# A small store of zeros to a scratch tensor, put on the DMA ring of the row stores

## Chip, cores, metric

One core of one Trainium2 chip. The metric is device time in microseconds (us), the median of several runs. All runs used here are of the fast state; repeats of one kernel mostly agree within 0.2%.

A ratio in this document is the mean time of one kernel's fast runs divided by the mean time of the other kernel's fast runs of the same rounds. It is therefore not quite the ratio of the medians that are quoted beside it. "Before" is run again in each set of rounds; its median was 165.10 to 165.27 us.

## The reference

Weights are adapted once (a low-rank update, then each column scaled to length `m`), and a large batch of rows is multiplied by them.

```python
batch, seq_len, in_dim, out_dim, rank = 16, 2048, 256, 256, 16
W_adapted = W + scale * (lora_A @ lora_B)
W_norm = np.sqrt(np.sum(W_adapted ** 2, axis=0, keepdims=True) + 1e-8)
W_final = W_adapted / W_norm * m
y = x.reshape(-1, in_dim) @ W_final          # 32768 x 256, float32
```

`x` and `y` are 33.6 MB each; the weights are small.

## The kernel before

Loads of W and x are issued by SyncE and go to one DMA ring (q1 in the profile). Loads of the small weights and all row stores are issued by ScalarE and go to another ring (q10). `x` comes in 8 blocks of 4 MB, 5 buffers deep; each partition's part of a block is one run of 32 KB.

```python
def load_x(b):                                    # SyncE's ring, q1
    t = xpool.tile([P, DJ, IN], FP32, name="x_sb", tag="x_sb")      # bufs=5
    nc.sync.dma_start(out=t, in_=x_flat[b * BLK : (b + 1) * BLK].rearrange("(p j) k -> p j k", p=P))
    return t

nc.scalar.dma_start(out=a_nat, in_=lora_A.rearrange("(c p) r -> p c r", p=P))   # ScalarE's ring, q10
nc.sync.dma_start(out=w_nat, in_=W.rearrange("(c p) o -> p c o", p=P))
nc.scalar.dma_start(out=b_nat, in_=lora_B)
nc.scalar.dma_start(out=m_row, in_=m[None, :])
# ... identity, ones, a warm-up of the square root table, then the weight chain:
nc.tensor.matmul(mb_ps, ones[0:1, :], m_row, start=True, stop=True)   # spreads m over the partitions
# ... lora_A @ lora_B, norm, w_final (bf16)

for b in range(NBLK):                             # 8 blocks
    x_sb = load_x(b)
    for c in range(DJ // J):                      # 8 chunks of a block
        # 8 transposes -> xt_ps; VectorE copies xt_ps to xt_sb (bf16); 8 matmuls -> y_ps
        nc.scalar.copy(out=x_sb[:, c * J : (c + 1) * J, :], in_=y_ps)      # result over the input
        if c + 1 in store_after[b]:               # after the block; thrice in the last one
            nc.scalar.dma_start(out=out_flat[...], in_=x_sb[:, j0:j_stored, :])   # q10 again
```

The sixth load of x needs the buffer of the first block, so it waits until the first row store has left. A row store goes out only when ScalarE has copied the block's last result.

## Time and profile before

| | before |
|---|---|
| time, median of 3 | 165.10 us |
| span of the profile | 163.3 us |
| bytes moved by DMA | 67.55 MB, 414 GB/s on average |
| busy share of TensorE, VectorE, ScalarE | 77%, 50%, 40% |
| last row store issued | 151.33 us |

The first view is the profile page of before: the mean busy share of the 16 DMA engines (tenths) and their rate in 40 slices of the span, and the DMA queues with packets, MB and their share of the time of 16 engines.

```profile
DMA  6999998999999899999999999999999999999992
GB/s 197 414 474 401 449 450 381 474 425 377 389 425 474 385 470 425 387 482 409 421 466 393 458 429 393 492 393 421 474 401 441 429 409 466 409 413 429 407 425 86
...
q1 hardware_dynamic: 1424, 33.82, 48.9%
q10 hardware_dynamic: 1746, 33.59, 48.0%
```

The engines of the DMA are at 9 (90% or more) almost from the start to the end, and two rings share them almost evenly. The table of windows says the same by stage (columns: window, length, busy time and count of each engine, TensorE clock, DMA share, GB/s):

```profile
17.00:151.00 134.00, 118.32 (x1012) 102.89 (x1010) 75.56 (x65) 63.83 (x64) 0.00 (x0) 1.00 1.00 427
151.00:163.00 12.00, 0.00 (x0) 0.00 (x0) 0.00 (x0) 0.30 (x1) 0.00 (x0) 0.65 0.74 313
```

Between 17 and 151 us the DMA share is 1.00, and TensorE is busy for 118 of 134 us. In the packet records of the trace one 32 KB packet takes 1.213 us at the median. Each engine has to move 64 of them in and the equivalent of 64 out: 128 x 1.213 = 155.3 us. That is an estimate of the floor of this kernel with these packets; the records of all its packets sum to 158.8 us per engine.

The chain of waits (shares of the span by engine, then by line) points elsewhere:

```profile
PE 57%; DVE 26%; DMA 4%; issue 2%; ACT 1%; DVEq 1%; ACTq 1%
```

It follows compute back from ScalarE's last copy. How far that is from the end of the kernel is shown by two fences: the timeline (start, length, engine, line, operation), then the table of DMA issues (count, KB each, us from issue to landing):

```profile
150.28 1.01 ACT L165 COPY x_sb<-y_ps 128x1024 f32<-128x1024 f32 x1
151.33 0.34 ACTq L170 DMA_DIRECT2D out_dram<-x_sb  x1
```

```profile
out_dram<-x_sb ACTq DMA_DIRECT2D x2, 1024.0 KB, 11.0
```

Compute ends at 151.3 us. The last two row stores, 1 MB each, take 11.0 us at the median to land, because other stores are still in the rings ahead of them: by the packet records 3.8 MB are moved after 151.33 us. Compute is ahead of the end of the stores by about 11 us, here called the backlog.

The start, from the timeline of before:

```profile
1.22 3.29 SPq L52 DMA_DIRECT2D x_sb<-in_x_dram  x5
1.78 0.53 ACTq L66 DMA_DIRECT2D m_row<-in_m_dram  x1
2.34 1.28 ACT L76 ACT_TABLE_LOAD   x1 [2.34 <-issue]
8.96 1.19 PE L91 MATMUL mb_ps<-m_row,ones 1*128 1x256 f32 x2 [4.58 <-DMA m_row<-in_m_dram]
14.03 3.67 PE L147 MATMUL xt_ps<-identity,x_sb 128*128 128x128 f32 x16
```

The bias row `m_row` is issued at 1.78 us and its matmul can begin only at 8.96 us: its packets take turns with 32 KB packets of x on the same engine.

### The profile page before, as it was taken

To read this page: it belongs to the slowest core of one execution; us is meant where nothing else is said; L and a number is where in the kernel's file an instruction comes from. 1 tells how busy PE (TensorE), PEld (TensorE's weight loads), DVE (VectorE), ACT (ScalarE), POOL (GpSimd) and SP (SyncE) were. 2 spreads that over 40 slices of the span, in tenths; PEclk is the share of its full clock that TensorE was granted. 3 is DMA by queue.
4 is the path that set the end of the run, shared out by engine and by line. 5 is a ranking of instruction groups with operands and counts; after the bars stand their busy time and mean duration, and the time that the engine had idled before them with its cause. 6 is when DMAs were issued, how large, how long until landed. Compare 5 with 4: busy or idle time off the path is not lost.

```text
span 163.3 us, 2370 instructions
## 1 busy us (share of the span) xinstructions
PE 125.4 (77%) x1034; PEld 107.9 (66%) x1034; DVE 81.1 (50%) x76; ACT 66.1 (40%) x67; POOL 0.7 (0%) x6
## 2 busy tenths in 40 slices
PE   0049888888888888888888888898889888886000
PEld 0028677777777777777778777777887777774000
DVE  0145755555555555554555455545554555455000
ACT  3001244443544444444444364427441844085000
POOL 1000000000000000000000000000000000000000
PEclk9999999999999999999999999999999999999955
DMA  6999998999999899999999999999999999999992
GB/s 197 414 474 401 449 450 381 474 425 377 389 425 474 385 470 425 387 482 409 421 466 393 458 429 393 492 393 421 474 401 441 429 409 466 409 413 429 407 425 86
DMA packets 3180, 67.55 MB, mean 414 GB/s; under 512 B 593, under 2 KB 866, under 8 KB 866
## 3 DMA queue, kind: packets, MB, share of 16 engines
q1 hardware_dynamic: 1424, 33.82, 48.9%
q10 hardware_dynamic: 1746, 33.59, 48.0%
q8 instruction: 8, 0.13, 0.3%
q14 instruction: 2, 0.02, 0.0%
HBM read 33.85 MB, written 33.55 MB: 413 GB/s over the span
## 4 chain that ended last, share of the span: by engine, by line
PE 57%; DVE 26%; DMA 4%; issue 2%; ACT 1%; DVEq 1%; ACTq 1%
PE y_ps L158 33%; DVE xt_sb L153 23%; PE xt_ps L147 22%; DMA m_row<-in_m_dram 4%; PE n_ps L115 1%; DVE rnorm L124 1%; DVEq L206 1%; PE mb_ps L91 1%; ACT x_sb L165 1%; DVE w_final L126 0%; DVE sq L110 0%; DVE wa L106 0%; ACTq L60 0%; ACTq L64 0%; ACT norm L119 0%
## 5 line engine op out<-in xcount | busy, mean ns | idle before, releaser
L153 DVE CAST xt_sb<-xt_ps 128x1024 bf16<-128x1024 f32 x64 | 75.4, 1220 | 56.6 <-PE xt_ps L147 42.2
L165 ACT COPY x_sb<-y_ps 128x1024 f32<-128x1024 f32 x64 | 64.1, 1013 | 72.5 <-PE y_ps L158 72.4
L158 PE MATMUL y_ps<-w_final,xt_sb 128*128 128x256 bf16 x512 | 65.5, 273 | 11.5 <-DVE xt_sb L153 11.5
L147 PE MATMUL xt_ps<-identity,x_sb 128*128 128x128 f32 x512 | 68.7, 279 | 3.4 <-DVE xt_sb L153 3.1
L147 PEld LDWEIGHTS xt_ps<-identity,x_sb 128*128 128x128 f32 x512 | 58.7, 144 | 7.8 <-DVE xt_sb L153 6.7
L158 PEld LDWEIGHTS <-xt_sb 128*128 128x128 bf16 x512 | 47.8, 98 | 22.8 <-DVE xt_sb L153 18.2
L91 PE MATMUL mb_ps<-m_row,ones 1*128 1x256 f32 x2 | 1.2, 694 | 4.6 <-DMA m_row<-in_m_dram 4.6
L119 ACT ACTIVATE norm<-n_ps,eps_col 128x256 f32<-128x256 f32 x1 | 0.5, 473 | 10.4 <-PE n_ps L115 10.4
L91 PEld LDWEIGHTS mb_ps<-m_row,ones 1*128 1x128 f32 x2 | 0.5, 304 | 5.0 <-DVE aT L88 5.0
L82 DVE CAST b_bf<-b_nat 16x256 bf16<-16x256 f32 x1 | 0.3, 280 | 6.5 <-DMA b_nat<-in_lora_B_dram 6.5
L86 PE MATMUL aT_ps<-identity,a_nat 128*16 128x128 f32 x2 | 0.6, 394 | 3.8 <-DMA a_nat<-in_lora_A_dram 3.8
L115 PE MATMUL n_ps<-sq,ones 128*128 128x256 f32 x4 | 2.1, 674 | 1.5 <-DVE sq L110 1.5
L124 DVE RECIPROCAL rnorm<-norm 128x256 f32<-128x256 f32 x1 | 1.8, 1753 | 2.0 <-ACT norm L119 2.0
L86 PEld LDWEIGHTS aT_ps<-identity,a_nat 128*16 128x16 f32 x2 | 0.1, 88 | 3.8 <-issue 3.8
L115 PEld LDWEIGHTS n_ps<-sq,ones 128*128 128x128 f32 x4 | 1.2, 323 | 2.2 <-DVE sq L110 2.0
L76 ACT ACT_TABLE_LOAD x1 | 1.3, 1283 | 2.3 <-issue 2.3
L93 DVE COPY m_all<-mb_ps 128x256 f32<-128x256 f32 x1 | 0.4, 424 | 2.1 <-PE mb_ps L91 2.1
L126 DVE TENSOR_TENSOR w_final<-wam,rnorm 128x256 bf16<-128x256 f32 x2 | 0.8, 424 | 0.0
L122 DVE TENSOR_TENSOR wam<-wa,m_all 128x256 f32<-128x256 f32 x2 | 0.8, 418 | 0.0
L110 DVE TENSOR_TENSOR sq<-wa 128x512 f32<-128x512 f32 x1 | 0.7, 693 | 0.0
L106 DVE SCALAR_TENSOR_TENSOR wa<-ab_ps,w_nat 128x512 f32<-128x512 f32 x1 | 0.7, 692 | 0.0
L97 PE MATMUL ab_ps<-b_bf,aT 16*128 16x256 bf16 x2 | 0.6, 416 | 0.0
(11 smaller groups left out, 2.0 us busy)
## 6 DMA issues: line engine op xcount, KB each, us to landing
x_sb<-in_x_dram SPq DMA_DIRECT2D x8, 4096.0 KB, 31.2
out_dram<-x_sb ACTq DMA_DIRECT2D x7, 4096.0 KB, 27.9
out_dram<-x_sb ACTq DMA_DIRECT2D x1, 2048.0 KB, 12.4
out_dram<-x_sb ACTq DMA_DIRECT2D x2, 1024.0 KB, 11.0
w_nat<-in_W_dram SPq DMA_DIRECT2D x1, 256.0 KB, 2.8
a_nat<-in_lora_A_dram ACTq DMA_DIRECT2D x1, 16.0 KB, 2.9
b_nat<-in_lora_B_dram ACTq DMA_DIRECT2D x1, 16.0 KB, 6.2
m_row<-in_m_dram ACTq DMA_DIRECT2D x1, 1.0 KB
```

The lines of the kernel that those rows point to most:

```text
L76: nc.scalar.activation(out=warm, in_=eps_col, func=AF.Sqrt)
L86: nc.tensor.transpose(aT_ps[:, c * P : (c + 1) * P], a_nat[:, c, :], identity)
L91: nc.tensor.matmul(mb_ps, ones[0:1, :], m_row, start=True, stop=True)
L115: nc.tensor.matmul(n2_ps, ones, sq[:, c, :], start=(c == 0), stop=(c == KC - 1))
L122: nc.vector.tensor_mul(out=wam[:, c], in0=wa[:, c], in1=m_all)
L124: nc.vector.reciprocal(out=rnorm, in_=norm)
L126: nc.vector.tensor_mul(out=w_final[:, c], in0=wam[:, c], in1=rnorm)
L147: nc.tensor.transpose(xt_ps[:, kc, j * P : (j + 1) * P], x_sb[:, c * J + j, kc * P : (kc + 1) * P], identity,)
L153: nc.vector.tensor_copy(out=xt_sb, in_=xt_ps)
L158: nc.tensor.matmul(y_ps[:, j, :], xt_sb[:, kc, j * P : (j + 1) * P], w_final[:, kc, :], start=(kc == 0 and (j % (J // 2)) == 0), stop=(kc ...
L165: nc.scalar.copy(out=x_sb[:, c * J : (c + 1) * J, :], in_=y_ps)
L206: with _tile.TileContext(nc) as tc:
```

## The change

An internal scratch tensor gets 128 rows of 64 B of zeros, stored by ScalarE just behind the load of `m_row`. Nothing reads it. The question is what a small extra DMA costs when it is put on a ring that later carries the row stores.

```diff
     nc.scalar.dma_start(out=b_nat, in_=lora_B)
     m_row = startup.tile([1, OUT], FP32)
     nc.scalar.dma_start(out=m_row, in_=m[None, :])
+
+    scratch = nc.dram_tensor("scratch", (P, 16), FP32, kind="Internal").ap()
+    mark = startup.tile([P, 16], FP32)
+    nc.vector.memset(mark, 0.0)
+    nc.scalar.dma_start(out=scratch, in_=mark)
```

## The prediction

> **What bounds the kernel now.** The DMA engines, not the compute. A table of windows gives a DMA share of 1.00 in every window from 17 to 151 us. The queue table splits it: 48.9% for the ring of the loads (q1), 48.0% for the ring of the row stores (q10). In the packet records a 32 KB packet takes 1.213 us at the median; each of 16 engines moves 64 of them for the loads and the equivalent of 64 for the stores: 128 x 1.213 = 155.3 us of a span of 163.3. The chain of waits names TensorE and VectorE instead, because it follows compute back from the last copy; but that copy ends at 151.3 us and 12 us follow in which only stores drain (last store issued at 151.33, landing 11.0 us later). So compute ends with a DMA backlog of 11 us: a few us of delay in compute are hidden.
>
> **What the change adds.** One VectorE memset of 128x16 (the 128x1 one took 0.06 us), one ScalarE DMA issue (0.49 to 0.53 us for its neighbours), and a store of 128 rows of 64 B: 8 small packets and a semaphore packet per engine. It removes nothing.
>
> 1. The ScalarE table load, at 2.34 us, moves by about 0.5 us. ScalarE's next need is at 14.19 us: free.
> 2. The store stands behind the bias-row load m_row; that still lands at about 8.8 us.
> 3. DMA time: 64 B reads of lora_A took 0.011 us each, semaphore packets 0.009: together 0.1 us of each engine. Writes may cost more: the Trainium skill (DMA: Bandwidth & Descriptors, Specifications) says that under 512 B the engine does read-modify-write; no run shows a small write yet. At 0.05 us each (what a 1 KB packet took) it would be 0.45 us, an estimate. As DMA is the limit, this counts in full.
> 4. The store takes turns with x packets (same page, Queues, rings and completion order: engines switch rings at packet boundaries). b_nat's data ran at about 4.5 us, its semaphore packets one x packet later. If each small packet takes a turn of 1.2 us, the store lands near 18 us; if all 8 go together, near 10. No one waits for it.
> 5. The rotation of DMA semaphores shifts by one. The fifth load of x would wait for lora_B (landed by 7.5 us) instead of W. Over 12 MB of loads are queued before it: free. Later reuse falls on transfers long landed.
>
> The row stores begin at 34.1 us, long after. What is left is the order of turns: one engine's last semaphore packet comes 1.16 us behind the next; another phase could move that end by some tenths of a us either way.
>
> **Predicted:** 165.3 us, 8 times in 10 between 164.7 and 166.1. Chances: faster by over 2% 0.01, within 2% 0.97, slower by over 2% 0.02.
>
> **Right, if** DMA share is still 1.00 between 17 and 151 us, 32 KB packets still take 1.213 us, m_row lands within 0.3 us of 8.8, the first x chunk starts at 14.0, compute ends at about 151.3, and the store's packets add under 0.5 us per engine. **Wrong, if** m_row or the first x load lands over 1 us later, a load of x is held up by the scratch store, or engines idle anew.
>
> **What would make it wrong.** The scratch tensor moving the outputs in memory so that packets take another time; 64 B writes that hold an engine for a microsecond each (+9 us); a semaphore shift that makes a load wait for a store in flight; or a phase shift worth more than 1.2 us.

## The result

| | before | after |
|---|---|---|
| median | 165.13 us (4 runs) | 165.17 us (4 runs) |
| ratio, 95% interval | | 1.000, 0.9983 to 1.0017 |
| span of the profile | 163.3 us | 163.4 us |
| `m_row` matmul starts | 8.96 us | 9.92 us |
| last row store issued | 151.33 us | 152.25 us |

The profile page of after, the same lines as of before:

```profile
DMA  6999999999999999899999999999999999999992
GB/s 197 430 474 386 465 433 393 477 409 377 393 397 489 393 457 437 385 483 409 413 465 393 473 421 393 481 411 413 465 401 449 437 401 465 417 413 417 421 413 88
...
q1 hardware_dynamic: 1424, 33.82, 48.9%
q10 hardware_dynamic: 1890, 33.60, 48.1%
```

q10 has 144 packets more: 128 rows and 16 semaphore packets. The windows:

```profile
17.00:151.00 134.00, 118.51 (x1016) 103.40 (x1014) 76.46 (x67) 63.00 (x63) 0.00 (x0) 1.00 1.00 427
151.00:163.00 12.00, 0.17 (x2) 0.00 (x0) 0.00 (x0) 1.11 (x2) 0.00 (x0) 0.62 0.75 320
```

The DMA share is 1.00 again and the rate 427 GB/s again. The packet records give 1.213 us as the median of a 32 KB packet, as before, and 0.011 us for each row of the scratch store, 0.09 us in all per engine.

The chain of waits of after is that of before but for 5% instead of 4% of DMA, the late `m_row`:

```profile
PE 57%; DVE 26%; DMA 5%; issue 2%; ACT 1%; DVEq 1%; ACTq 1%
```

The start, the last copy, the last row store and the landing of the scratch store (timeline, then table of DMA issues):

```profile
1.22 6.77 SPq L52 DMA_DIRECT2D x_sb<-in_x_dram  x5
2.35 0.36 ACTq L73 DMA_DIRECT2D scratch<-mark  x1
2.74 1.28 ACT L83 ACT_TABLE_LOAD   x1 [2.74 <-issue]
9.92 1.19 PE L98 MATMUL mb_ps<-m_row,ones 1*128 1x256 f32 x2 [5.54 <-DMA m_row<-in_m_dram]
14.91 3.15 PE L154 MATMUL xt_ps<-identity,x_sb 128*128 128x128 f32 x16
...
151.21 1.01 ACT L172 COPY x_sb<-y_ps 128x1024 f32<-128x1024 f32 x1
152.25 0.34 ACTq L177 DMA_DIRECT2D out_dram<-x_sb  x1
```

```profile
scratch<-mark ACTq DMA_DIRECT2D x1, 8.0 KB, 17.1
out_dram<-x_sb ACTq DMA_DIRECT2D x2, 1024.0 KB, 10.1
```

Three things are to be seen. The scratch store took 17.1 us to land. The five loads of x take until 7.99 us to issue instead of 4.51 (start plus length of the merged line), as the fifth waits for `lora_B`. And all of compute came 0.9 to 1.0 us later than before, from the matmul of `m_row` to the last row store, yet the kernel ended at the same time: the backlog at the end took it up.

The late `m_row` was not predicted. It had to be tested whether the store causes it.

### The profile page after: what moved, and what is told of

The parts are those of the page before. It is cut to its first block, busy times and chain, and to the rows that moved or that the text cites. A ratio compares the mean times of both kernels' runs of the same rounds, so it can differ in the third digit from the quotient of the medians.

```text
span 163.4 us, 2373 instructions
## 1 busy us (share of the span) xinstructions
PE 124.8 (76%) x1034; PEld 107.8 (66%) x1034; DVE 81.1 (50%) x77; ACT 66.1 (40%) x67; POOL 0.7 (0%) x6
## 4 chain that ended last, share of the span: by engine, by line
PE 57%; DVE 26%; DMA 5%; issue 2%; ACT 1%; DVEq 1%; ACTq 1%
PE y_ps L165 33%; DVE xt_sb L160 23%; PE xt_ps L154 22%; DMA m_row<-in_m_dram 5%; PE n_ps L122 1%; DVE rnorm L131 1%; DVEq L213 1%; PE mb_ps L98 1%; ACT x_sb L172 1%; DVE w_final L133 0%; DVE sq L117 0%; DVE wa L113 0%; ACTq L60 0%; ACTq L64 0%; ACT norm L126 0%
```

## The experiments

Theory D: the DMA engines are the limit, so added DMA time counts in full, and delays of compute count only beyond the backlog, which was taken to be some 11 us (too much, as will be seen). Rival C: the chain of waits is right, compute is the limit, and every microsecond of a late weight chain counts. Beside these, theories L and S on the late `m_row`, and theories on what small packets do to the ring.

### The two kernels again

The kernel before and the change, unedited, each against before.

> The change itself again, unedited, for its noise and for one question: in the first profile of the change the bias row m_row landed 0.97 us later than before (start of its matmul 9.92 us instead of 8.96). Theory L (lottery): the engine that carries m_row was one of the few whose lora_B packet came one x packet late, which is decided before the scratch store is on the ring, so in a repeat the matmul can start near 8.9 or near 9.9. Theory S (store): the scratch store makes it late, so it starts at 9.7 to 10.1 again. Both: ratio 0.998 to 1.003, 165.1 us, since the delay is absorbed by the DMA backlog at the end.

> The kernel before, unedited, against itself, with a second profile: how far the start of m_row's matmul moves without any scratch store (8.96 us in the first profile). Theory L: it can be anywhere from 8.9 to 10 us. Theory S: 8.8 to 9.1 us. Time ratio 0.998 to 1.002.

Measured: the change again 165.22 us (ratio 0.9998, 0.9985 to 1.0011), before again 165.27 us (0.9999, 0.9985 to 1.0013). The timeline of the change again:

```profile
8.89 1.19 PE L98 MATMUL mb_ps<-m_row,ones 1*128 1x256 f32 x2 [4.18 <-DMA m_row<-in_m_dram]
...
151.22 0.34 ACTq L177 DMA_DIRECT2D out_dram<-x_sb  x1
```

With the same code the matmul started at 8.89 us, and the last row store was issued at 151.22 us instead of 152.25. Before again had its matmul at 9.19 us. In the six other profiles with a scratch store behind `m_row` on that ring, described below, it started at 8.78, 9.11, 8.91, 8.91, 8.71 and 8.83 us. Only one of eight such profiles is near 9.9, so theory S falls: the store does not delay `m_row` by 1 us. In the packet records of the first profile of the change, `m_row`'s own packet ran at 8.09 us instead of 6.9 to 7.2 us as in the other seven and in the first profile of before, one turn with an x packet later. That fits theory L: the packet follows by 1.22 us a semaphore packet of `lora_B` at 6.87 us, one of three late ones of 16, and such late packets occur without the store too (three in the first profile of before, none in the second). What decides which engine is late was not tested, nor whether the store makes a late one more frequent.

The two profiles of the change are also a test of theory D by accident: compute ended 1.03 us apart, and the profiled executions took 165.18 and 165.14 us.

### The store ahead of the bias row

```diff
     nc.scalar.dma_start(out=b_nat, in_=lora_B)
+    scratch = nc.dram_tensor("scratch", (64, 16), FP32, kind="Internal").ap()   # (128, 16) in ahead_full
+    mark = startup.tile([64, 16], FP32)                                         # [128, 16] in ahead_full
+    nc.vector.memset(mark, 0.0)
+    nc.scalar.dma_start(out=scratch, in_=mark)
     m_row = startup.tile([1, OUT], FP32)
     nc.scalar.dma_start(out=m_row, in_=m[None, :])
```

> The store, cut to 64 rows of 64 B, is issued ahead of m_row instead of behind it, so that m_row waits on the ring for 4 small packets and a semaphore packet, 5 turns of 1.22 us = 6.1 us. Both theories: m_row's matmul starts at about 15 us instead of 8.96, and the last row store is issued at about 157.4 us instead of 151.3. Theory D (the DMA engines are the limit, 11 us of backlog at the end of compute): the time stays within 0.5% of before, 164.9 to 165.9 us, and the tail after the last copy shrinks from 12 to about 6 us. Theory C (the chain of waits is right, compute is the limit): +6 us, about 171 us.

> The full 8 KB store ahead of m_row: 9 turns, about 11 us. m_row's matmul starts at about 20 us, the last row store is issued at about 162.3 us. Theory D: the backlog of about 11 us is used up; the last 1 MB store needs some 2.4 us of transfer plus about 2 us of issue and landing, so the time is about 168 to 170 us (+2 to +3%). Theory C: +11 us, about 176 us. If small packets took no turns, m_row would not move at all and the time would be 165.1 us.

| | `m_row` matmul starts | last row store issued | median | ratio, 95% interval |
|---|---|---|---|---|
| before (first profile) | 8.96 us | 151.33 us | 165.23 us | |
| half, 4 rows per engine | 13.93 us | 157.85 us | 166.13 us | 1.0050, 1.0023 to 1.0077 |
| full, 8 rows per engine | 18.71 us | 161.04 us | 169.84 us | 1.0302, 1.0268 to 1.0335 |

Of the half version, its matmul of `m_row`, its last row store and the landing of the last two row stores (timeline, then DMA issues):

```profile
13.93 1.19 PE L96 MATMUL mb_ps<-m_row,ones 1*128 1x256 f32 x2 [9.46 <-DMA m_row<-in_m_dram]
...
157.85 0.34 ACTq L175 DMA_DIRECT2D out_dram<-x_sb  x1
```

```profile
out_dram<-x_sb ACTq DMA_DIRECT2D x2, 1024.0 KB, 6.1
```

The windows of the full version, then its matmul of `m_row`, its last row store and the landings in the same way:

```profile
17.00:151.00 134.00, 116.12 (x966) 101.10 (x967) 75.52 (x68) 58.62 (x59) 0.00 (x0) 1.00 0.97 412
151.00:163.00 12.00, 7.99 (x69) 6.44 (x67) 4.71 (x4) 5.98 (x6) 0.00 (x0) 0.98 0.93 392
```

```profile
18.71 1.19 PE L96 MATMUL mb_ps<-m_row,ones 1*128 1x256 f32 x2 [14.24 <-DMA m_row<-in_m_dram]
...
161.04 0.34 ACTq L175 DMA_DIRECT2D out_dram<-x_sb  x1
```

```profile
out_dram<-x_sb ACTq DMA_DIRECT2D x2, 1024.0 KB, 6.2
```

What stands behind small packets on a ring waits for them, by turns: 9 turns (8 rows and a semaphore packet) cost `m_row` 9.8 us, 5 turns cost 5.0 us, so 1.0 to 1.1 us for a turn on average. In the packet records a turn with an x packet is 1.22 us; one turn, at about 13.0 us, falls to the short semaphore packet of the first load of x instead, so both delays are about 1 us less than expected. The order of the change (behind `m_row`) is what made it free. Of 6.5 us by which the end of compute moved in the half version, 0.9 us reached the time; of 9.7 us in the full version, 4.6 us did. Rival C asked for all of it, so C falls, and a backlog is shown. But it hid only 5.6 and 5.1 us, not 11. The fences say why: with compute late, the last two row stores still took 6.1 and 6.2 us at the median to land, so some 5 of the 11.0 us were usable (11.0 - 6.1 = 4.9, an estimate from these landings). In the full version the DMA share in the window from 17 to 151 us falls to 0.97: the engines now wait for compute at times.

The half version missed the expected range by 0.2 us, and its runs spread from 165.33 to 166.91 us. Counting in the packet records how many of the 16 engines are busy, the engines idle 0.55 us on average from 133 to 143 us, where before they idle not at all. So some of the backlog is needed earlier than at the very end. That spread from run to run is open.

### The same store on the other ring, and as one packet

`sp_ring` issues the store from SyncE, ahead of the first load of x. `one_packet` keeps it on ScalarE's ring but shapes the same 8 KB as 16 rows of 512 B, one packet per engine.

```diff
-    nc.scalar.dma_start(out=scratch, in_=mark)
+    nc.sync.dma_start(out=scratch, in_=mark)                 # sp_ring
```

```diff
-    scratch = nc.dram_tensor("scratch", (P, 16), FP32, kind="Internal").ap()
-    mark = startup.tile([P, 16], FP32)
+    scratch = nc.dram_tensor("scratch", (16, 128), FP32, kind="Internal").ap()   # one_packet
+    mark = startup.tile([16, 128], FP32)
```

> The same 8 KB store on the other ring, that of the loads, between W and the first load of x. There are no x packets ahead of it with which to take turns. If turns made it land 17.1 us after issue, it lands here within 5 us of issue; if small writes to memory are slow in themselves, it lands late here too. The first load of x may move by some tenths of a us. Time 164.8 to 165.6 us, same.

> The same 8 KB laid out as 16 rows of 512 B: one packet and one semaphore packet per engine, 2 turns instead of 9. Landing about 8.5 us earlier than in the change: some 8 us after issue instead of 17.1. Time the same, 164.8 to 165.5 us, as nobody waits for it.

The landings, first of sp_ring, then of one_packet (tables of DMA issues):

```profile
scratch<-mark SPq DMA_DIRECT2D x1, 8.0 KB, 2.9
```

```profile
scratch<-mark ACTq DMA_DIRECT2D x1, 8.0 KB, 8.7
```

The landing is 2.9 us where no x packet is in the way, 8.7 us with 2 turns, 17.1 us with 9 turns (16.1 us in the change again, where `m_row` was not late). A small write to memory is not slow by itself here; the turns make it late. The Trainium skill (DMA: Bandwidth & Descriptors, Queues, rings and completion order) says that an engine changes between rings at packet boundaries. This agrees, and it shows that each 64 B row was a packet of its own: in the records of the change, successive rows on one engine start about 1.22 us apart.

The time of one_packet was 165.03 us (ratio 0.9987, 0.9974 to 1.0001), the same. The time of sp_ring was 166.56 us (ratio 1.0065, 1.0037 to 1.0093), outside its expected range, although the weights now came early. Its timeline:

```profile
1.72 3.47 SPq L52 DMA_DIRECT2D x_sb<-in_x_dram  x5
4.54 1.22 PE L98 MATMUL mb_ps<-m_row,ones 1*128 1x256 f32 x2
15.46 3.67 PE L154 MATMUL xt_ps<-identity,x_sb 128*128 128x128 f32 x16 [5.70 <-DMA x_sb<-in_x_dram]
```

The matmul of `m_row` starts 4.4 us earlier than before and gains nothing, as theory D says. But the first load of x is issued 0.5 us later (1.72 instead of 1.22 us), and the first chunk of x starts 1.4 us later (15.46 instead of 14.03). By the packet records the engines idled 0.55 us on average in the 10 us after the first x packet, where before they did not idle, and the 32 KB packets took 0.5 us more per engine in all. So the likely cause is a late start of the DMA, which a backlog of stores at the end cannot cover; that this makes the whole rise was not shown. Why the runs spread from 165.33 to 166.85 us is open.

### The dose by bytes

```diff
-    scratch = nc.dram_tensor("scratch", (P, 16), FP32, kind="Internal").ap()
-    mark = startup.tile([P, 16], FP32)
+    scratch = nc.dram_tensor("scratch", (P, 1024), FP32, kind="Internal").ap()   # wide_4k: 512 KB
+    mark = startup.tile([P, 1024], FP32)
```

> The dose by bytes: 512 KB again, but as 128 rows of 4 KB: 8 packets per engine of about 0.155 us (half of the 0.309 us of an 8 KB packet) in place of 8 of 0.011. Theory D: +1.2 us minus what was there, 166.1 to 166.6 us, 0.6 to 0.9% slower. If there is slack on the DMA engines: no change, 165.1 us.

Measured: 166.38 us against 165.25 (ratio 1.0067, 1.0054 to 1.0081). The DMA queues of its page:

```profile
q1 hardware_dynamic: 1424, 33.82, 48.6%
q10 hardware_dynamic: 1890, 34.11, 48.5%
```

The 8 packets of each engine took 0.159 us each at the median, 1.27 us in all by the records; the medians differ by 1.13 us. Here the added DMA time counts in full within the noise, as theory D says, and there is no slack on the DMA engines. Compute also ended 0.9 us later than before (last row store issued at 152.19 us), but in the first profile of the change the same delay cost nothing.

### The dose by packets

The 64 B of zeros per partition are stored k times, to a scratch tensor k times as large: 8k small packets per engine. The first of these runs was `many_64`.

```diff
-    scratch = nc.dram_tensor("scratch", (P, 16), FP32, kind="Internal").ap()
+    scratch = nc.dram_tensor("scratch", (P, 64, 16), FP32, kind="Internal").ap()     # k = 64; also 16, 8, 3
-    nc.scalar.dma_start(out=scratch, in_=mark)
+    nc.scalar.dma_start(out=scratch, in_=mark[:, None, :].to_broadcast([P, 64, 16]))
```

> The dose by packets: the scratch tensor is 128 x 64 rows of 64 B (512 KB), the same 64 B of zeros per partition stored 64 times, so 512 small packets per engine instead of 8. Theory D with the cost seen (11 ns a packet, 13 ns pitch where two ran back to back): +6.7 us, about 171 to 173 us. If a 64 B write holds an engine for 0.05 us (read-modify-write felt by the engine): +25 us. The packets take turns with x packets until the first five loads are done at about 48 us, so the first row store, in order behind them on the ring, moves little before about 50 us instead of starting at 34.

> The dose by packets again, a quarter of it: 16 rows of 64 B per partition, 128 small packets per engine. With 64 rows the time rose by 14.3 us, twice the 6.7 us expected, and ScalarE's issue of the first row store took 24.0 us instead of 0.37. Theory B (blocked issue): the packets cost about 13 ns each, and the rest came from ScalarE standing still in that issue, so that compute ended 19 us late. Then 128 packets cost 1.6 us (166.6 to 167.2 us) as long as the issue of the first row store stays under 1 us; if that issue takes many us too, the time goes up by more. Theory P (packets cost more than they show, about 28 ns each): +3.5 us, about 168.7 us, with the last row store issued at about 151 us.

> 8 rows of 64 B per partition: 64 small packets per engine. At 34.1 us some 42 of them are left, and they take turns with x packets until the loads end at about 51 us. Either way the first row store cannot move before that. Theory Q (waiting in the ring costs little, only a held ScalarE costs): if the issue of the first row store is not held (0.4 us), compute ends at about 151 us and the time is 165.5 to 167 us; if it is held until about 51 us as with 16 and 64 rows, compute ends at about 163 us and the time is 171 to 173 us. Theory W (the wait of the row store behind small packets is itself the cost): 171 to 173 us also where the issue is not held.

> 3 rows of 64 B per partition: 24 small packets and a semaphore packet per engine, 25 turns of 1.22 us from about 7 us, so the last one runs at about 38 us, just past 34.1 us, where ScalarE issues the first row store. That store then waits a few us on the ring behind the small packets. Expected: the time stays within 0.5% of before, 165.0 to 166.0 us, because the loads of x fill the engines meanwhile. If the issue itself is held, ScalarE stands still for up to 4 us and compute ends up to 4 us later, which the backlog of 11 us still covers.

| k | small packets per engine | issue of the first row store takes | last row store issued | median | ratio, 95% interval |
|---|---|---|---|---|---|
| 1 (the change) | 8 | 0.37 us | 152.25 us | 165.17 us | 1.0000, 0.9983 to 1.0017 |
| 3 | 24 | 0.38 us | 151.06 us | 165.30 us | 1.0008, 0.9996 to 1.0020 |
| 8 | 64 | 0.39 us | 151.20 us | 165.32 us | 1.0012, 0.9999 to 1.0025 |
| 16 | 128 | 17.26 us | 163.63 us | 172.73 us | 1.0453, 1.0429 to 1.0477 |
| 64 | 512 | 24.02 us | 170.82 us | 179.54 us | 1.0860, 1.0836 to 1.0883 |

ScalarE's timeline around its first row store, first with k = 8, then with k = 16:

```profile
33.98 0.39 ACTq L177 DMA_DIRECT2D out_dram<-x_sb  x1
35.85 1.01 ACT L172 COPY x_sb<-y_ps 128x1024 f32<-128x1024 f32 x1 [1.90 <-PE y_ps L165]
```

```profile
34.06 17.26 ACTq L177 DMA_DIRECT2D out_dram<-x_sb  x1
51.42 1.93 ACT L172 COPY x_sb<-y_ps 128x1024 f32<-128x1024 f32 x2 [17.39 <-issue]
```

The issue of the scratch store itself, with k = 16, then with k = 64:

```profile
2.34 0.59 ACTq L73 DMA_DIRECT2D scratch<-mark  x1
```

```profile
2.35 0.58 ACTq L73 DMA_DIRECT2D scratch<-mark  x1
```

With k = 8 the row store is issued in 0.39 us and ScalarE goes on copying. The store itself moves its first packet only at 52.5 us, by the packet records, where before that was at 37.7 us, because it stands behind small packets that take turns with x. This wait of 15 us costs nearly nothing (+0.1%): the loads of x fill the engines meanwhile. With k = 16 the issue instruction lasts 17.26 us, to 51.32 us. By then nearly all packets of the first five loads of x had started; 87 of 128 small packets per engine were still left, and most of them went at once from 52 to 53 us. With k = 64 the issue ended only at 58.08 us, when the small packets were down to 5 of 512. ScalarE copies nothing in that time, compute ends 12.3 us later than before (163.63 against 151.33), and the backlog is spent. So a wait in the ring is free here and a held ScalarE is not. Theory B (blocked issue) and theory Q say the same. Theory P (28 ns for each packet) and theory W (the ring wait is the cost) fall: k = 8 shows both 64 packets and the ring wait for 0.1%. In its records the small packets take 0.7 us per engine; less than that reached the time (0.07 us, at most 0.4 by the interval), and part of it ran at once with other packets of the same engine. The run with k = 3 does not test the wait: its small packets were done at 34.1 us, not at about 38 as expected.

The Trainium skill (Perfetto Trace Analysis, DMA Instruction — HWDGE) says that the instruction lasts until all of its descriptors have been generated, and that there is a buffer for them which can fill. A full buffer could explain a held issue, but this agrees only in part. By that account the scratch store itself, with its many rows, should be the long instruction; yet its issue took 0.58 us with k = 8 and k = 64 and 0.59 us with k = 16, and the hold fell on the next DMA that ScalarE issued. When that was issued, at about 34 us, 39 small packets per engine were left with k = 8 (not held), 103 with k = 16 and 487 with k = 64 (held). If the number left is what counts, the limit lies between 39 and 103. The ends of the two held issues (87 left, 5 left) don't fit one count, and what exactly is full stays open.

The sum for k = 16, per engine and from the packet records, against before: small packets 1.4 us, idle 4.9 us more, 32 KB packets 1.4 us more; 7.7 us together, for a rise of 7.5 us from the first x packet to the last packet (some packets of one engine run at once, so such sums come out a little high). For k = 64 the expectation of 6.7 us had left out the held issue, and the measured rise was 14.3 us: by the records small packets 8.9 us (a mean of 17 ns, a median of 11), of which some 3.7 us at once with other packets of the same engine, idle 7.9 us more, 32 KB packets 1.4 us more. Why the 32 KB packets took longer is open. The backlog hid about 5 us here too: compute ended 12.3 and 19.5 us later, the time rose by 7.5 and 14.3 us.

### The many packets from GpSimd

```diff
-    nc.scalar.dma_start(out=scratch, in_=mark[:, None, :].to_broadcast([P, 64, 16]))
+    nc.gpsimd.dma_start(out=scratch, in_=mark[:, None, :].to_broadcast([P, 64, 16]))   # many_64_pool
```

> The store of 512 small packets per engine issued from GpSimd, on neither of the two rings, so that no row store stands behind it and ScalarE cannot be held by it. Theory B: ScalarE's issue of the first row store stays near 0.37 us at about 34 us, compute ends at about 151 us, and the time rises by the packets alone, by 5.6 to 6.7 us if they are as small as on the ScalarE ring (171 to 172 us), or less if this path joins them. Theory P: again about +14 us.

Measured: 167.68 us against 165.19 (ratio 1.0147, 1.0128 to 1.0166). ScalarE's issue took 0.38 us again, and the last row store was issued at 153.46 us instead of 170.82. That is theory B's part that a store on a third ring cannot hold ScalarE. The price of 512 small packets could not be read from it, since this path joined them: the records show 128 packets of 4096 B on a ring of its own, 0.226 us each at the median, 1.76 us per engine. This is most of the 2.5 us; GpSimd's issue also lasted 2.83 us and the first chunk of x started at 16.03 us instead of 14.03, which was not taken apart further.

## Why the prediction was right, point by point

The measured 165.17 us lies 0.13 us from the predicted 165.3, and the class (within 2%) was right. The interval of 0.3 us either way is too wide to tell the lower forecast cost of 0.1 us from none; its size is judged by the packet records (point 4).

1. The bound. Right, and shown: wide_4k turned 1.27 us of added packets into 1.13 us of time, while in the half version of the store ahead of the bias row a delay of 6.5 us at the end of compute became only 0.9 us. "A few us of delay in compute are hidden" was right as worded: about 5 us are, not the 11.
2. The table load of ScalarE moved from 2.34 to 2.74 us and nobody waited. Right.
3. "That still lands at about 8.8 us" was wrong for the profiled run (its matmul started 0.96 us later), and right for the change: in the seven other profiles with a store behind `m_row` it started at 8.71 to 9.11 us. The criterion "within 0.3 us" was too tight for one profile, and so were those for the first x chunk (14.91 us instead of 14.0) and the end of compute (152.25 instead of 151.3), which followed `m_row`; in the repeat they were 14.02 and 151.22. That the unforeseen 1 us cost nothing was no luck: the prediction's hidden backlog covers it. A delay of 1 us in one profile is not an effect of the edit until a repeat shows it.
4. The size of the DMA time. The lower figure was right: 0.011 us per row, 0.09 us per engine. The Trainium skill (DMA: Bandwidth & Descriptors, Specifications) says that below 512 B the engine does read-modify-write; whatever the memory does, the engines did not feel 0.05 us per row. With 64 rows per engine that would have been 3.2 us, and many_8 rose by 0.07 us in the medians, at most 0.4 us by its interval.
5. The turns. Right: the store landed at 19.4 us (2.35 + 17.1) and in the repeat at 18.4 us (2.35 + 16.1), against "near 18"; 9 packets, 9 turns.
6. The shift of semaphores. Right in its effect: the fifth load of x was issued at 7.66 us instead of 4.05, waiting for `lora_B`, and nothing came of it. No load waited for the scratch store. "Later reuse falls on transfers long landed" was not quite so: SyncE waited 5.8 us for the first load of x before the sixth, which had to wait for a row store until 59.5 us anyway (59.55 us, before 59.51).

What the prediction had not seen is how near the same edit stands to a cost: issued one load earlier, ahead of `m_row`, it costs 3%, and with 128 small packets per engine instead of 8 it costs 4.5% by holding ScalarE.

## What to carry to other kernels

When 16 DMA engines are busy throughout, ask for an added transfer first how many engine-microseconds its packets take, and then what stands behind it: on the same ring (one small packet, one turn with a large one), and behind its issue on the same engine. The chain of waits follows compute; compare its end with the end of the stores before believing that compute is the limit, and do not take the whole gap for slack (here 5 of 11 us). Repeat a profile before explaining a shift of a microsecond at the start.

## What the Trainium skill lacked or had wrong

- DMA: Bandwidth & Descriptors (Queues, rings and completion order) describes a packet as typically 9 to 17 descriptors. On ScalarE's ring each 64 B row was a packet of its own with a turn of its own: 8 rows and a semaphore packet held up what stood behind them by 9.8 us.
- The same page (Specifications) warns of read-modify-write below 512 B and gives no cost of it for a store. Here a 64 B store row took an engine 0.011 us, as a 64 B load row did, and 64 of them per engine moved the time by 0.1%.
- Perfetto Trace Analysis (DMA Instruction — HWDGE) has a DMA instruction last until all of its descriptors are generated, and mentions a buffer that can fill, but not how many fit. Here the issue of the store with the many rows lasted 0.58 us with 64 and with 512 small packets per engine, and the next DMA issued by the same engine was held: its issue took 0.39 us where 64 had been put on the ring ahead of it, 17.26 us with 128, and 24.02 us with 512.
- DMA: Bandwidth & Descriptors (Specifications) gives about 27 GiB/s for one engine, which is 29 GB/s. Here a 32 KB packet took 1.213 us at the median, which works out at 27.0 GB/s for one engine and 432 GB/s for 16, for loads and stores alike; the windows from 17 to 151 us show 427 GB/s.
